# Probabilities transposed two blocks at a time, first loads in turn, and a priority for the norms' mean squares in a two-layer hybrid decoder

## The chip, the cores and the metric

The kernel runs on one NeuronCore of one Trainium2 chip. The metric is the device time of one execution in microseconds (us). A core has five engines that work from queues of their own and wait for each other by semaphores: TensorE (PE: matmuls and transposes; PEld: its weight loads), VectorE (DVE), ScalarE (ACT), GpSimd (POOL) and SyncE (SP), which here issues nearly all loads. An engine's queue runs in order: an instruction that waits holds up everything behind it on that engine. Matmuls write to PSUM, a small memory that ACT and DVE read; everything else lies in SBUF.

## The reference

Two layers, each on 256 positions of width 1024, everything in float32:

```
h = rmsnorm(x);  z = h @ w_in                       # 14 column groups
y_a = nsa(z...) @ w_up_nsa                          # 8 heads, 2 groups: compressed,
                                                    # selected and window branch
y_b = retention(z...) @ w_up_ret                    # 4 heads
x = x + (sigmoid(ma) * y_a + sigmoid(mb) * y_b) @ w_out
x = x + relu(rmsnorm(x) @ w_ff1)**2 @ w_ff2
x = x + sigmoid(rmsnorm(x) @ w_ple_gate) * (p @ w_ple)
```

In the nsa part each of the three branches has a softmax of its own over masked scores, p = e / sum(e), is multiplied by a gate, and the weighted values of the branches are added. With 256 positions the selected branch sees every block, so it is causal attention, and so is the window.

## The kernel before

**Arithmetic.** A float32 matmul is done as three matmuls of a faster type: each operand is split into a high part (`hi`, `XH`, written by ACT) and a rest (`lo`, `XL`, written by DVE as operand minus high part). A weight tile of 128x1024 arrives as `raw`, is split into `hi` and `lo`, and gives 24 matmuls of 256 columns (or 12 of 512).

**Order.** The order on TensorE is written out by the program itself: a main thread takes weight tiles one after the other from a plan and multiplies them ("bulk" below), and background generators (`attend`, `collect`) push small pieces of attention in between. Each piece says by `yield` at which time of a simple model of the engines its inputs should be there; the piece is put on TensorE at the next `poke()` after that. Nothing of this is checked at run time: what is not ready when TensorE comes to it stalls TensorE. On ACT, DVE and POOL a scheduler of the tile library sets the order, and puts instructions under `tc.high_priority()` earlier where it can.

**Attention.** A softmax is done for a pair (g, t) of a head group and a half of the positions, in the order (0,0), (0,1), (1,0), (1,1). `softmax` makes scores (`sc`), exponentials (`e`) and, on POOL, scales `e` block by block with the gate over the sum. `weigh` then takes the blocks (3 for t = 0, 5 for t = 1, one of them only 16 wide, which goes to the tile `PC`). For block i:

- `turn(i)` transposes the four heads' probabilities on TensorE into a PSUM tile `pt` (4 flips). ACT copies it into a tile `pp` (high part), and DVE subtracts that from `pt` into another `pp` (rest).
- `apply(i)` multiplies both `pp` tiles with the values into the accumulator `ot`.

There are two `pt` buffers in turn, so a turn can start only when the DVE subtraction of the turn two before it has read its tile. There are four `pp` buffers, two a block. After the last `apply`, ACT and DVE add the branches up (`o`), and split them (`NHh`, `NHl`). When all four pairs are weighed, `retain` does the last part of retention (`rV`, `rs`, flips of `tmp`).

**Start.** `unit_load` loads the weight tiles; the first tile (plan entry 0) comes in two pieces, and ahead of the first piece stands one load of the first two chunks of x (`XT`). `unit_split(0)` splits, for each piece, one chunk of x and then the piece.

**Norms.** `finish_a` sums squares on TensorE, makes the mean `ms` on DVE and its power `r` on POOL; `finish_b` flips `r` on TensorE.

Of the kernel before, what the change touches and what calls it, by code (L numbers as in the profile page):

```python
# [12 lines left out]
ALU = mybir.AluOpType  # L13
# [4 lines left out]
D = 1024  # L18
# [6 lines left out]
EPS = 1e-6  # L25
# [86 lines left out]
def trunk(ctx: ExitStack, tc: tile.TileContext, xT, wu, wg, cst, msk, par, pin, out):  # L112
# [31 lines left out]
    def p_tile(shape):  # L144
        return ps.tile(shape, F32, tag="pt", name=nm("pt"), bufs=2)

    def o_tile(shape):
        return ps.tile(shape, F32, tag="ot", name=nm("ot"), bufs=1)

    def tmp(shape, dt=F32, tag="tmp", bufs=NTMP):  # L150
        return tp.tile(shape, dt, tag=tag, name=nm(tag), bufs=bufs)
# [7 lines left out]
    def small(shape, tag, bufs=2):  # L159
        return sp.tile(shape, F32, tag=tag, name=nm(tag), bufs=bufs)  # L160
# [3 lines left out]
    cur = [0.0]  # L164

    def width(ap):
        n = 1
        for d in ap.shape[1:]:
            n *= d
        return n  # L170
# [5 lines left out]
    def charge(eng, us):  # L176
        us += 0.03
        if first[0]:
            cur[0] += us + 0.6
            return  # L180
        gs = gaps[eng]
        while len(gs) > 1 and gs[0][1] < vt["pe"] - 6.0:
            gs.pop(0)
        for i, (a, e) in enumerate(gs):
            s = max(a, cur[0])
            if s + us <= e:
                new = []
                if s - a > 0.15:
                    new.append([a, s])
                if e - s - us > 0.15:  # L190
                    new.append([s + us, e])
                gs[i:i + 1] = new
                break
        vt[eng] = gs[-1][0]
        cur[0] = s + us + 0.06

    def fresh(t=None):
        cur[0] = vt["pe"] if t is None else t
# [4 lines left out]
    def act(o, *a, **k):  # L203
        charge("act", 0.1 + width(o) / 1200)
        return nc.scalar.activation(o, *a, **k)  # L205

    def tt(**k):
        charge("dve", 0.07 + width(k["out"]) / 960)
        return nc.vector.tensor_tensor(**k)  # L209

    def ts(**k):
        charge("dve", 0.07 + width(k["out"]) / 960)
        return nc.vector.tensor_scalar(**k)  # L213
# [13 lines left out]
    def gp(**k):  # L227
        n = width(k["out"])
        assert k["op"] in (ALU.pow, ALU.mult, ALU.add)
        charge("pool", (1.1 if n <= 4 else 2.6) if k["op"] == ALU.pow else 0.14 + n / 310)  # L230
        return nc.gpsimd.tensor_tensor(**k)  # L231

    def mm(o, a, b_, **k):
        n = width(b_)
        vt["pe"] += max(n, 64) / 2400 * (4 if b_.dtype == F32 else 1)
        fresh()
        return nc.tensor.matmul(o, a, b_, **k)  # L237

    def flip(o, a, i):
        vt["pe"] += 0.107  # L240
        fresh()
        return nc.tensor.transpose(o, a, i)  # L242

    def sub(out_, a, b):
        tt(out=out_, in0=a, in1=b, op=ALU.subtract)
# [39 lines left out]
    def load_x(a, b_):  # L285
        nc.sync.dma_start(XT[:, a:b_, :], xT[:, a:b_, :])
# [21 lines left out]
    def pair_load(l, i):  # L308


        j = sum(k not in PLAIN for k in range(i))
        B = bp.tile([P, 2, 2, 512], F32, tag=(f"S{2 * l + 1}", f"S{2 * l + 2}", "S7")[j % 3], name="pair")
        for k in range(2):
            nc.sync.dma_start(B[:, k].rearrange("p a b -> p (a b)"), wu[BIG_IX[(l, "ff2", 2 * i + k)]])
        T = bp.tile([P, 3, 512], F32, tag=f"S{5 + j % 2}", name="tsum")
        pairs[l, i] = B, T
# [15 lines left out]
    def unit_load(i):  # L332
        key = PLAN[i]
        if key[1] in PAIR:
            if key[1] == "s2a":
                pair_load(key[0], key[2])
            return
        if key in TWIN:
            h, tag = TWIN[key]
            if h == 0:  # L340
                state["twin"] = bp.tile([P, 2, NW], F32, tag=tag, name=f"raw{i}")
            t = state["twin"][:, h]
        elif key[1] == "w1" or key in EXTRA:
            tag = EXTRA.get(key) or ("B1", "B2", "B5", "B6")[key[2] % 4]
            t = bp.tile([P, NW], F32, tag=tag, name=f"raw{i}")
        else:
            t = wp.tile([P, NW], F32, tag="raw", name=f"raw{i}", bufs=RAW)
        w = spans[i] = 560 if key[1] == "kvg" else NW
        src = wg[KVG_IX[key]] if key[1] == "kvg" else wu[BIG_IX[key]]
        m = w // PIECES.get(key, 1)  # L350
        for c in range(0, w, m):
            if i == 0 and c == 0:
                load_x(0, 2)
            nc.sync.dma_start(t[:, c:c + m], src[:, c:c + m])
        raws[i] = t

# [28 lines left out]
    def advance(i):  # L385
        n = len(PLAN)
        while state["load"] < n and ring[state["load"]] < ring[min(n, i + AHEAD)] + RAW and (
                state["load"] < i + AHEAD + RAW + XA):
            unit_load(state["load"])
            state["load"] += 1  # L390
            load_early(state["load"])
        split_to(i)
# [41 lines left out]
    LATE = 0.9  # L434
# [82 lines left out]
    def finish_a(st):  # L517
        sq = st["sq"]
        pr = p_tile([P, 2])
        for t in range(2):  # L520
            mm(pr[:, t:t + 1], sq[:, 0, t * P:(t + 1) * P], ones, start=True, stop=True)
        ms = small([P, 2], "ms")
        ts(out=ms, in0=pr, scalar1=1.0 / D, scalar2=EPS, op0=ALU.mult, op1=ALU.add)
        r = small([P, 2], "r")
        gp(out=r, in0=ms, in1=mhalf[:, :2], op=ALU.pow)
        st["r"] = r
# [54 lines left out]
    def layer(l, st):  # L581
# [193 lines left out]
        def weigh(g, t):  # L775
            e, blocks, scaled = es.pop((g, t))

            n = len(blocks) - 1
            ot = o_tile([P, HG, P])
            parts = {}  # L780

            def turn(i):
                o, w, b, vv = blocks[i]
                pt = p_tile([P, HG, P])
                for h in range(HG):
                    flip(pt[:w, h, :], e[:, h, o:o + w], ident)
                if w == P:
                    ph = tmp([P, HG, P], F32R, tag="pp", bufs=4)
                    pl = tmp([P, HG, P], F32R, tag="pp", bufs=4)
                else:  # L790
                    ph, pl = PC[:, 0], PC[:, 1]
                act(ph[:w], pt[:w], AF.Copy)
                sub(pl[:w], pt[:w], ph[:w].bitcast(F32))
                parts[i] = ph, pl

            def apply(i):
                o, w, b, vv = blocks[i]
                ph, pl = parts.pop(i)
                mm(ot, vv, ph.rearrange("p a b -> p (a b)"), start=i == 0, stop=False)
                mm(ot, vv, pl.rearrange("p a b -> p (a b)"), start=False, stop=i == n)  # L800

            fin = []
            yield scaled[0]
            turn(0)
            fin.append(cur[0])
            for i in range(1, n + 1):
                yield scaled[i]
                fresh()
                turn(i)
                fin.append(cur[0])  # L810
                yield fin[i - 1]
                apply(i - 1)
            yield fin[n] + LATE
            apply(n)
            on = o2 = tmp([P, 2, P], tag="o", bufs=1)
            ov = ot.rearrange("p (c two) q -> p c two q", two=2)
            act(o2[0:64], ov[64:128, :, 0, :], AF.Copy)
            act(o2[64:128], ov[0:64, :, 1, :], AF.Copy)
            tt(out=on[0:64], in0=ov[0:64, :, 0, :], in1=o2[0:64], op=ALU.add)
            tt(out=on[64:128], in0=ov[64:128, :, 1, :], in1=o2[64:128], op=ALU.add)  # L820
            freed.append(cur[0])
            nh = NHh[:, 2 * g:2 * g + 2, t * P:(t + 1) * P]
            act(nh, on, AF.Copy)
            sub(NHl[:, 2 * g:2 * g + 2, t * P:(t + 1) * P], on, nh.bitcast(F32))
            weighed.add((g, t))
# [173 lines left out]
        for name, u in SEQ[l]:  # L999
# [7 lines left out]
            elif name == "fa":  # L1007
                positions()
                finish_a(st)
                r = st["r"]  # L1010
                rh = small([P, 2], "rh")
# [6 lines left out]
            elif name == "fb":  # L1018
# [3 lines left out]
                    op0=ALU.mult, op1=ALU.mult)  # L1022
# [27 lines left out]
            else:  # L1050
                if name in ("rq", "rk"):
                    i, hp = ("rq", "rk").index(name), u // 2
# [10 lines left out]
                for t in range(2):  # L1063
# [4 lines left out]
                    else:  # L1068
# [4 lines left out]
                            op0=ALU.add, op1=ALU.mult)  # L1073
# [189 lines left out]
        for u in range(2):  # L1263
            for i in range(2):
                b_unit(pms[i], take(l, "fh", 2 * i + u), XH, XL, 4 * u, u == 0, u == 1)
                if u == 1:
                    for q in range(2):
                        ff1_end(2 * i + q, pms[i][:, q])
        finish_a(stf)
        r2 = small([P, 2], "r2")  # L1270
        for i in range(15):
# [39 lines left out]
        for u in range(2):  # L1311
# [3 lines left out]
            for n in range(2):  # L1315
                pm = mm_tile([P, 2, S])
                for k in range(2):
                    for q in range(2):
                        c = (2 * n + q) * P
                        three(pm[:, q, :], vh[:, k, c:c + P], vl[:, k, c:c + P], ph[:, k, :],  # L1320
                              pl[:, k, :], k == 0 and q == 0, k == 1 and q == 1)
                c = 4 * u + 2 * n
# [180 lines left out]
```

## Time and profile before

| | |
|---|---|
| median of 3 runs | 836.47 us (835.97 to 837.29) |
| the profiled execution | 834.93 us |
| its span, first to last instruction | 832.8 us |
| TensorE busy | 823.4 us, 99% of the span |
| VectorE busy | 704.5 us, 85% |
| ScalarE busy | 572.1 us, 69% |
| GpSimd busy | 70.5 us, 8% |

A timeline row has: start (us from the span's start), duration, engine, line, operation, out<-in, shapes, count; in brackets the idle time of the engine before it and what ended it. A row can stand for several equal instructions in a row (x4), and its duration is then from the first start to the last end. Matmuls overlap: one of 256 columns is shown as about 0.28 us long, but the next starts about 0.12 us later; only the distance of the starts tells TensorE's pace. TensorE idle time under 0.15 us is not shown as idle.

### The profile page before, as it was taken

The numbers are of one execution on the slowest core, as the hardware profiler recorded it, in microseconds if no ns is written. First come the engines' busy times: TensorE is split into PE (matmuls) and PEld (weight loads), VectorE is DVE, ScalarE is ACT, GpSimd is POOL, SyncE is SP. The second block draws the span as 40 slices with busy tenths as digits, with TensorE's granted clock in tenths as the row PEclk, the third lists the DMA queues.
The fourth block names the chain that finished last, engine by engine and source line by source line (L and its number), as shares of the span: only waits on it lengthen the run. The fifth ranks groups of instructions, "written<-read, shape, count | busy, mean of one in ns | idle before, by whom it ended". The sixth has DMA issues, their size and how long they took to land.

```text
span 832.8 us, 15190 instructions
## 1 busy us (share of the span) xinstructions
PE 823.4 (99%) x5841; PEld 768.8 (92%) x5841; DVE 704.5 (85%) x1155; ACT 572.1 (69%) x992; POOL 70.5 (8%) x66
## 2 busy tenths in 40 slices
PE   8999999999999999999999999999999999999997
PEld 7998899999999999998999989999999999999897
DVE  7897888787989797979888978886879988989695
ACT  7895977554767676768579868765457677767662
POOL 0410241010000000000003004121000000000000
PEclk9999999999999999999999999999999999999999
DMA  8776453466437474725565654446663565657132
GB/s 319 279 275 211 128 162 127 159 230 240 160 134 245 145 240 148 237 92 203 183 205 172 211 193 135 131 136 205 199 227 129 199 204 178 227 165 239 50 106 74
DMA packets 43560, 152.02 MB, mean 183 GB/s; under 512 B 5088, under 2 KB 5856, under 8 KB 43488
## 3 DMA queue, kind: packets, MB, share of 16 engines
q1 hardware_dynamic: 43344, 151.04, 53.8%
q8 instruction: 46, 0.75, 0.4%
q14 instruction: 26, 0.21, 0.1%
q10 hardware_dynamic: 144, 0.01, 0.0%
HBM read 149.99 MB, written 1.05 MB: 181 GB/s over the span
## 4 chain that ended last, share of the span: by engine, by line
PE 98%; DMA 0%; DVE 0%; ACT 0%; POOL 0%; issue 0%; DVEq 0%; POOLq 0%
PE mm L237 62%; PE sc L237 15%; PE pt L237 10%; PE ot L237 9%; PE pt L242 3%; DMA par<-in_par_dram 0%; PE sc L242 0%; POOL r L231 0%; ACT XH L205 0%; DVE lo L209 0%; ACT hi L205 0%; DVE gz L217 0%; DVE gz L209 0%; DVE XT L209 0%; ACT gz L205 0%
## 5 line engine op out<-in xcount | busy, mean ns | idle before, releaser
L205 ACT ACTIVATE hi<-raw 128x1024 fp32r<-128x1024 f32 (+2 forms) x241 | 248.0, 1041 | 152.7 <-PE mm L237 96.2
L209 DVE TENSOR_TENSOR lo<-raw,hi 128x1024 fp32r<-128x1024 f32 (+2 forms) x241 | 292.3, 1225 | 47.6 <-ACT hi L205 46.7
L237 PE MATMUL mm<-XH,hi 128*128 128x256 f32 x992 | 284.1, 286 | 0.0
L237 PE MATMUL mm<-XH,lo 128*128 128x256 f32 x992 | 280.1, 282 | 0.0
L237 PE MATMUL mm<-XL,hi 128*128 128x256 f32 x992 | 279.1, 281 | 0.0
L237 PEld LDWEIGHTS mm<-XH,hi 128*128 128x128 f32 x992 | 187.1, 189 | 4.4
L237 PEld LDWEIGHTS mm<-XL,hi 128*128 128x128 f32 x992 | 187.2, 189 | 4.2
L237 PEld LDWEIGHTS mm<-XH,lo 128*128 128x128 f32 x992 | 186.9, 188 | 0.0
L209 DVE TENSOR_TENSOR lo<-pair,hi 128x1024 fp32r<-128x1024 f32 x44 | 53.8, 1222 | 14.3 <-ACT hi L205 13.7
L205 ACT ACTIVATE hi<-pair 128x1024 fp32r<-128x1024 f32 x44 | 46.2, 1050 | 16.9 <-PE mm L237 16.5
L231 POOL TENSOR_TENSOR r<-ms,mhalf 128x2 f32<-128x2 f32 x6 | 5.4, 903 | 513.7 <-DVE ms L213 513.7
L209 DVE TENSOR_TENSOR lo<-tsum,hi 128x1024 fp32r<-128x1024 f32 (+1 forms) x44 | 42.0, 954 | 6.4 <-ACT hi L205 6.3
L205 ACT ACTIVATE hi<-tsum 128x1024 fp32r<-128x1024 f32 (+1 forms) x44 | 37.0, 840 | 14.3 <-PE pt L237 9.0
L231 POOL TENSOR_TENSOR e<-e,acf 128x512 f32<-128x512 f32 (+1 forms) x32 | 36.9, 1182 | 113.6 <-DVE acf L209 75.5
L237 PE MATMUL mm<-hi,XH 128*128 128x512 f32 (+2 forms) x128 | 44.4, 347 | 0.0
L237 PE MATMUL mm<-lo,XH 128*128 128x512 f32 (+2 forms) x128 | 43.6, 341 | 0.0
L237 PE MATMUL mm<-hi,XL 128*128 128x512 f32 (+2 forms) x128 | 43.6, 341 | 0.0
L205 ACT ACTIVATE e<-e,nmx 128x128 f32<-128x128 f32 (+2 forms) x96 | 37.6, 393 | 7.4 <-DVE nmx L225 7.4
L205 ACT ACTIVATE ah<-aq 128x896 fp32r<-128x896 f32 (+1 forms) x32 | 29.2, 912 | 11.4 <-DVE aq L209 11.4
L231 POOL TENSOR_TENSOR rso<-rsv,mhalf 128x2 f32<-128x2 f32 (+3 forms) x18 | 25.1, 1398 | 119.5 <-DVE rsv L213 119.4
L209 DVE TENSOR_TENSOR al<-aq,ah 128x896 fp32r<-128x896 f32 (+1 forms) x32 | 33.5, 1046 | 1.9 <-ACT ah L205 1.8
L237 PE MATMUL pt<-hi,ah 128*128 128x512 f32 x84 | 33.2, 395 | 0.0
(226 smaller groups left out, 1767.5 us busy)
## 6 DMA issues: line engine op xcount, KB each, us to landing
raw<-in_wu_dram SPq DMA_DIRECT2D x231, 512.0 KB, 3.9
pair<-in_wu_dram SPq DMA_DIRECT2D x44, 512.0 KB, 4.8
raw<-in_wg_dram SPq DMA_DIRECT2D x8, 280.0 KB, 4.3
cst<-in_cst_dram SPq DMA_DIRECT2D x1, 768.0 KB, 7.5
out_dram<-XT SPq DMA_DIRECT2D x3, 256.0 KB, 2.6
XT<-in_xT_dram SPq DMA_DIRECT2D x2, 256.0 KB, 4.5
raw<-in_wu_dram SPq DMA_DIRECT2D x2, 256.0 KB, 4.2
XT<-in_xT_dram SPq DMA_DIRECT2D x1, 512.0 KB, 6.9
```

The costliest lines, as they stand in the source:

```text
L205: return nc.scalar.activation(o, *a, **k)
L209: return nc.vector.tensor_tensor(**k)
L231: return nc.gpsimd.tensor_tensor(**k)
L237: return nc.tensor.matmul(o, a, b_, **k)
L242: return nc.tensor.transpose(o, a, i)
```

## The change

Three edits.

```
--- unit_load
-            if i == 0 and c == 0:
-                load_x(0, 2)
+            if i == 0:
+                load_x(c // m, c // m + 1)
--- finish_a
-        ts(out=ms, in0=pr, scalar1=1.0 / D, scalar2=EPS, op0=ALU.mult, op1=ALU.add)
+        with tc.high_priority():
+            ts(out=ms, in0=pr, scalar1=1.0 / D, scalar2=EPS, op0=ALU.mult, op1=ALU.add)
--- weigh
-            fin = []
-            yield scaled[0]
-            turn(0)
-            fin.append(cur[0])
-            for i in range(1, n + 1):
-                yield scaled[i]
-                fresh()
-                turn(i)
-                fin.append(cur[0])
-                yield fin[i - 1]
-                apply(i - 1)
-            yield fin[n] + LATE
-            apply(n)
+            fin, last = 0.0, []
+            for i in range(0, n + 1, 2):
+                now = range(i, min(i + 2, n + 1))
+                yield scaled[now[-1]]
+                for j in now:
+                    fresh()
+                    turn(j)
+                due_, fin = fin, cur[0]
+                if last:
+                    yield due_
+                    for j in last:
+                        apply(j)
+                last = now
+            yield fin + LATE
+            for j in last:
+                apply(j)
```

Before, a turn was followed by the apply of the block before it; now two turns are queued together, and the applies of the two blocks before them come after that. The turns of a pair thus go (0 1)(2) or (0 1)(2 3)(4). The instructions are the same in number and shape, but for one more load. Over both layers the order on TensorE changes in the attention stretches alone, and on ACT and DVE there and at the start.

TensorE, the turns of the pair (0,0) in the first layer, before (`pt` is written by the flips, `mm` is bulk, `sc` scores, `ot` an apply):

```order
L242 MATMUL pt_1226<-cst,e_1082 128x128 x4
L237 MATMUL mm_1108<-hi_1069,XH_100 128x512
L237 MATMUL mm_1108<-lo_1070,XH_100 128x512
L237 MATMUL mm_1108<-hi_1069,XL_101 128x512
L242 MATMUL pt_1238<-cst,e_1082 16x128 x4
...
L237 MATMUL sc_1251<-KT_162,qT_169 128x272 x2
L237 MATMUL sc_1254<-KT_162,qT_169 128x256 x2
L237 MATMUL ot_1156<-pp_1231,V_163 128x512
L237 MATMUL ot_1156<-pp_1232,V_163 128x512
L242 MATMUL pt_1273<-cst,e_1082 128x128 x4
```

The same place now:

```order
L242 MATMUL pt_1227<-cst,e_1083 128x128 x4
L242 MATMUL pt_1236<-cst,e_1083 16x128 x4
L237 MATMUL mm_1109<-hi_1070,XH_100 128x512
L237 MATMUL mm_1109<-lo_1071,XH_100 128x512
L237 MATMUL mm_1109<-hi_1070,XL_101 128x512
L242 MATMUL pt_1246<-cst,e_1083 128x128 x4
```

The third turn, which reuses the first turn's `pt`, stood behind six more bulk matmuls, a head's scores and the first apply; now three bulk matmuls lie between the second turn and it, and it has a wait of its own for DVE's subtraction of the first.

DVE, between the last apply of (0,1) and the first subtraction of (1,0), before (`o` and `NHl` belong to (0,1), `lo` is a weight split):

```order
L209 TENSOR_TENSOR lo_1769<-raw_1596,hi_1768 128x1024
L209 TENSOR_TENSOR o_1712<-ot_1376,o_1712 64x256 x2
L209 TENSOR_TENSOR pp_1732<-pt_1726,pp_1731 128x512
L209 TENSOR_TENSOR NHl_166<-o_1712,NHh_165 128x2x128
L225 ISA e_1539,nmx_1540<-sc_1741,masks,nq_171 128x256
```

The same place now:

```order
L209 TENSOR_TENSOR o_1660<-ot_1338,o_1660 64x256 x2
L209 TENSOR_TENSOR lo_1753<-raw_1559,hi_1752 128x1024
L209 TENSOR_TENSOR NHl_167<-o_1660,NHh_166 128x2x128
L209 TENSOR_TENSOR pp_1680<-pt_1674,pp_1679 128x512
L209 TENSOR_TENSOR PC<-pt_1683,PC 16x512
```

The weight split and `NHl` now stand between `o` and the subtraction, where before `o` was followed by it.

SP, the first loads, before:

```order
L286 DMA XT<-in_xT_dram 128x512
L354 DMA raw_102<-in_wu_dram 128x512 x2
L354 DMA raw_106<-in_wg_dram 128x560
L286 DMA XT<-in_xT_dram 128x512
L354 DMA raw_109<-in_wu_dram 128x1024
```

The same now:

```order
L286 DMA XT<-in_xT_dram 128x256
L354 DMA raw_102<-in_wu_dram 128x512
L286 DMA XT<-in_xT_dram 128x256
L354 DMA raw_102<-in_wu_dram 128x512
L354 DMA raw_107<-in_wg_dram 128x560
L286 DMA XT<-in_xT_dram 128x512
L354 DMA raw_110<-in_wu_dram 128x1024
```

One load of two chunks became two of one chunk, each ahead of the piece that goes with it, and everything behind stands one place later.

## Rows read from the trace of the kernel before

**Rows 1.** The page's first part: busy us, share of the span, instructions.

```profile
PE 823.4 (99%) x5841; PEld 768.8 (92%) x5841; DVE 704.5 (85%) x1155; ACT 572.1 (69%) x992; POOL 70.5 (8%) x66
```

**Rows 2.** Who TensorE waited for: us in total, times, longest.

```profile
PE pt L242 <- POOL r L231: 1.5, 1, 1.5
PE sc L237 <- ACT hi L205: 1.5, 1, 1.5
```

**Rows 3.** Chain that ended last, two unbroken pieces (256 and 512 columns): start, us.

```profile
173.63 12.81 PE mm L237 x108
25.27 5.59 PE sc L237 x24
```

**Rows 4.** Busy time by stretch; before the DMA share stands the granted clock.

```profile
85.00:130.00 45.00, 45.00 (x328) 42.22 (x327) 38.15 (x111) 36.82 (x110) 13.15 (x11) 1.00 0.44 137
400.00:412.00 12.00, 10.51 (x89) 10.31 (x89) 9.03 (x14) 5.77 (x8) 1.06 (x1) 1.00 0.78 257
```

**Rows 5.** In order of time, (0,0): two turns, then the first's copy and subtraction.

```profile
93.65 0.60 PE L242 MATMUL pt<-cst,e 128*128 128x128 f32 x4
94.78 0.60 PE L242 MATMUL pt<-cst,e 128*16 128x128 f32 x4
...
95.43 0.58 ACT L205 ACTIVATE pp<-pt 128x512 fp32r<-128x512 f32 x1
...
96.04 0.69 DVE L209 TENSOR_TENSOR pp<-pt,pp 128x512 fp32r<-128x512 f32 x1 [0.23 <-ACT pp L205]
```

**Rows 6.** In order of time, (1,0): a turn whose copy found ACT idle.

```profile
136.99 0.60 PE L242 MATMUL pt<-cst,e 128*128 128x128 f32 x4
...
137.69 0.60 ACT L205 ACTIVATE pp<-pt 128x512 fp32r<-128x512 f32 x1 [0.20 <-PE pt L242]
...
138.32 0.69 DVE L209 TENSOR_TENSOR pp<-pt,pp 128x512 fp32r<-128x512 f32 x1
```

**Rows 7.** In order of time, (1,1): the last apply, and what ACT and DVE do then.

```profile
161.23 0.62 PE L237 MATMUL ot<-pp,V 128*128 128x512 f32 x2
...
161.89 0.77 ACT L205 ACTIVATE o<-ot 64x256 f32<-64x256 f32 x2 [2.06 <-PE ot L237]
162.69 1.06 ACT L205 ACTIVATE hi<-raw 128x1024 fp32r<-128x1024 f32 x1
...
164.19 0.42 DVE L209 TENSOR_TENSOR NHl<-o,NHh 128x256 fp32r<-128x256 f32 x1
164.52 1.22 DVE L209 TENSOR_TENSOR lo<-raw,hi 128x1024 fp32r<-128x1024 f32 x1
```

**Rows 8.** DVE in order of time; two heads' masked scores fill 115.17 to 116.57.

```profile
113.89 1.37 DVE L209 TENSOR_TENSOR pp<-pt,pp 128x512 fp32r<-128x512 f32 x2
115.17 0.34 DVE L225 CUSTOM_DVE_ANT_0 e<-sc,masks,nq 128x128 f32<-128x128 f32 x1
...
116.57 1.22 DVE L209 TENSOR_TENSOR lo<-raw,hi 128x1024 fp32r<-128x1024 f32 x1
```

**Rows 9.** In order of time, retention's second set of flips, and what they read.

```profile
172.11 1.14 DVE L217 SCALAR_TENSOR_TENSOR tmp<-tmp,rso,rG 128x128 f32<-128x128 f32 x4 [0.90 <-POOL rso L231]
...
172.70 0.93 PE L242 MATMUL pt<-cst,tmp 128*128 128x128 f32 x4
```

**Rows 10.** In order of time, the start.

```profile
1.51 3.35 PE L237 MATMUL mm<-warm 128*128 128x512 f32 x7 [1.51 <-DVE warm L280]
4.84 0.91 ACT L205 ACTIVATE XH<-XT,par 128x256 fp32r<-128x256 f32 x2 [2.17 <-DMA par<-in_par_dram]
6.32 0.49 PE L237 MATMUL sc<-hi,XH 128*128 128x512 f32 x1 [1.45 <-ACT hi L205]
10.17 3.04 DVE L209 TENSOR_TENSOR lo<-raw,hi 128x1024 fp32r<-128x1024 f32 x3
11.49 0.46 PE L237 MATMUL sc<-lo,XH 128*128 128x512 f32 x1
11.79 0.39 PE L237 MATMUL sc<-hi,XL 128*128 128x512 f32 x1
```

**Rows 11.** In order of time, the norm before the gate of the first layer.

```profile
408.01 0.15 DVE L213 TENSOR_SCALAR ms<-pt 128x2 f32<-128x2 f32 x1
409.42 0.43 PE L242 MATMUL pt<-cst,r 128*128 128x128 f32 x2 [1.49 <-POOL r L231]
```

## The prediction

> **What bounds the kernel now.** First the page's busy line, which names the engine to look at: TensorE is busy for 99% of the span, the next engine for 85% [rows 1]. Then the list of what TensorE waited for: two waits of 1.5 us and nothing else of that size [rows 2], one at the start, one ahead of a flip of `r`. Then the chain of waits, where the reader sees long unbroken pieces of matmuls; they give TensorE's pace: 12.81 / 108 = 0.119 us for a matmul of 256 columns, 5.59 / 24 = 0.233 for one of 512 [rows 3]. The windows say that in the stretch with all four attention pairs TensorE is busy 45.00 of 45 us at a granted clock of 1.00, its upper level of 2.4 GHz, while VectorE and ScalarE are busy for 38.15 and 36.82 [rows 4]. So a wait that TensorE is spared is worth little, since nearly none is left, and every new wait of TensorE is added whole to the time: no slack lies behind it. The other two engines have 15% and 18% free, but in pieces: what they owe TensorE comes late whenever a longer work stands ahead of it in their queues.
>
> **The norms' mean squares.** `ms` is given a priority, but the instructions of VectorE and GpSimd keep their order around all six of them, so nothing moves: the 1.49 us ahead of the flip of `r` [rows 11] stay. Cost 0. Were it moved ahead as far as it can go, the gain would be that wait at most, and it occurs once.
>
> **First loads.** The first chunk of x now lands alone, and the first piece of weights one place sooner; TensorE's first real matmul, at 6.32, is released by ScalarE's split of a weight piece, behind the split of both chunks of x, 0.91 us for the two [rows 10]. So it may start some 0.45 sooner, half of that. But the same splits of ScalarE must be done before VectorE's `lo` rows, 10.17 to 13.21, and TensorE is at 11.49 and 11.79 already held to their pace: its matmul with `lo` is followed after 0.30 us instead of 0.233 [rows 3, 10]. The second piece, one issue later, keeps its place. What is won at 6.32 is lost by 11.5: 0, with ends of -0.45 (all of it kept) and +0.3 (one more issue in front of everything, the difference being as large as one such gap). The later loads that changed places are of no use before their tiles' splits, many us on: 0, and if that cover failed it would show as a wait for a DMA, which no row of [rows 2] has.
>
> The Trainium skill, page "Perfetto Trace Analysis", section "DMA Optimizations", has two rules for this that pull apart: split transfers let some of them start and finish sooner, while small ones carry more overhead. The first would make the time 0.45 us shorter; by the rows neither decides, because the pace at 11.49 is set elsewhere.
>
> **Turns, what is removed.** Two turns side by side could be cheaper than two apart if the change between flips and bulk had a price. From one turn to the next are 1.13 us, and three matmuls of 512 columns lie between [rows 5]: 1.13 - 3 x 0.233 = 0.43 us for four flips and both changes. I take 0.44 for a turn, side by side or apart. Gain 0.
>
> **Turns, what is added.** There are two `pt`. The third turn of a pair cannot start before VectorE has subtracted the first turn's tile. Before, the apply of that block stood ahead of it in the queue and had waited already, with bulk in between; now only a few matmuls lie between, and TensorE's queue stands still if the subtraction is late: all bulk behind it waits. The cost of each place is the end of that subtraction less the time at which TensorE gets there. The quickest release on record: turn at 136.99, copy at 137.69 with ScalarE waiting for it, subtraction from 138.32 to 139.01, so 2.02 us from a turn's start [rows 6]. Two subtractions in a row end 0.64 apart (115.17 - 113.89 = 1.28 for two [rows 8]).
>
> (0,0), order (0 1) (2): ScalarE and VectorE keep their order up to the first subtraction, which ends at 96.04 + 0.69 = 96.73 [rows 5]. TensorE reaches the third turn after two turns and three matmuls of 512: 93.65 + 2 x 0.44 + 0.70 = 95.23. Wait: **1.5 us**. This is the surest term. If both engines were idle it would still be 2.02 - 1.58 = 0.44.
>
> (0,1), order (0 1) (2 3) (4): TensorE reaches the third turn after 0.88 + 12 x 0.119 = 2.3 us. VectorE has ahead of the first subtraction a copy of `z`, released by a bulk result that ends 13 matmuls (1.55 us) before the first turn, then a weight split, a head's masked scores and another split. A split takes 1.2, two heads' scores 1.40, so one head's 0.7 [rows 8]; with 0.64 for each evacuation the subtraction ends -1.55 + 0.64 + 1.2 + 0.7 + 1.2 + 0.64 = 2.83 us after the turn's start: 0.55 late. The fourth turn, right behind, waits for the second subtraction, some 0.85 later, while its own flips would be reached 0.44 later: 0.4 more. **0.9**, from 0 (nothing ahead on VectorE: 2.02 against 2.3) to 1.8 (one more split of 1.2, less what the fourth turn no longer waits).
>
> (1,0), (0 1) (2): six matmuls ahead of its first turn lies the last apply of (0,1), and VectorE now does a weight split and `NHl` ahead of the first subtraction. The same sequence stands in the rows of (1,1): from the apply's start at 161.23, ScalarE begins `o` 0.66 later, the split's high part 1.46 later and ends it 2.52 later, VectorE ends the low part (1.2) at about 3.75, `NHl` (0.42) at 4.15, and the subtraction (0.64) at 4.8 [rows 7]. TensorE gets to the third turn after the apply's two matmuls, six of bulk, two turns, six of bulk and a head's scores (as long as four matmuls of 256): 0.47 + 0.71 + 0.88 + 0.71 + 0.49 = 3.25. That is 1.55; ScalarE may be held by a head's exponentials beforehand, about as long as VectorE's 0.7, which would make it 2.25. I take **1.8** (1.5 to 2.4, or 0 if the high part of the split goes behind the copy).
>
> (1,1), (0 1) (2 3) (4): the third turn is reached after 0.88 + 0.71 = 1.59 us. No weight split stands ahead of the subtraction, so the quickest release of 2.02 holds [rows 6]: 0.43, and the fourth turn 0.2 behind it (2.66 against 2.46). **0.6** (0.43 to 1.2, if a split comes first after all).
>
> **Retention.** TensorE's second flips of `tmp` take 0.93 instead of 0.60 since VectorE's four products are behind [rows 9]. VectorE has the pair's last work out of the way sooner now, and the flips come later: **-0.3** (-0.33 to +0.3).
>
> Other things moved are hidden: the gate's factors and GpSimd's scaling of a later pair come behind one or two weight splits, 2.4 us, against turns that follow over 10 us later; if that cover failed it would cost the same 2.4 once a pair.
>
> **Sum.** Per layer 1.5 + 0.9 + 1.8 + 0.6 - 0.3 = 4.5, two layers alike: +9.0 us. The profiled execution, 834.93 us (2.1 more than its span), becomes 843.9; it lies 1.5 below the median of the runs, so for the median 836.47 + 9.0 = **845.5 us**. Low end: (0,0) and (1,0) at 1.5 each and (1,1) at 0.43, the others at nothing, -0.3, with the start at -0.45: 2 x 3.1 - 0.45 = 5.8; I go to +4.5, since the copies of a batch could change places on ScalarE. High end: 1.6 + 1.8 + 2.4 + 1.2 + 0.2 = 7.2 per layer, +14.4.
>
> **Rivals.** 0.2% of this time, about 1.7 us, is what a measurement of this kernel can tell from no change.
>
> *Only the two sure places stall.* The scheduler's order leaves (0,1) and (1,0) covered: (1.5 + 0.6 - 0.1) x 2 = +4, 840.5 us. Against it: both have weight splits ahead of the subtraction. Chance 0.06.
>
> *The evacuations keep up.* If the copy and subtraction of each first turn come as fast as at idle engines, (0,0) waits 0.44 and (1,1) 0.43 a layer, the other two nothing: +1.7, less 0.6 for retention and some of the start: +0.7, 837.2, not slower by what can be told. The point from which it decides: the first subtraction ends within about 2 us of its turn's start. For it: [rows 6] shows such a release. Against it: [rows 5] shows one of 3.1 us, at the very place, with the same order ahead. Chance 0.05.
>
> *A gain.* Batches save a change between flips and bulk, the start is 0.45 sooner for good, the 1.49 us wait goes, and no turn waits: 836.47 - 1.9 = 834.5, or less. Against it: 0.43 per turn already without a batch, and an order around `ms` that does not change. Chance 0.02. The Trainium skill would speak for the first part: page "Perfetto Trace Analysis", section "Matmul Optimizations", says that the matmul engine scales its power with use, so matmuls are to be issued back to back in batches. The trace shows a granted clock of 1.00 over the whole stretch [rows 4] with turns apart, so there is nothing left to raise.
>
> *The clock falls.* If each of some eight waits dropped TensorE to its lower level, 1.2 GHz, for as long as the warm-up ran (seven matmuls in 3.35 us instead of 1.63 [rows 3, 10]), that is 1.7 each: +9 + 14 = 859. Against it: the stretch around the existing wait of 1.49 us keeps 1.00 [rows 4]. Chance 0.05.
>
> **How the numbers follow.** The forecast with its own bounds has 0.82, from 841.0 to 850.9. That leaves out the clock, the fast evacuations, the gain and the lower part of the second case, under 0.2 together, so the range stays there. Faster by over 0.2%: 0.02; within 0.2%: 0.05; slower: 0.93.
>
> **What would show it.** In the profile after, TensorE's list of waits should have a new first entry, flips into `pt` that waited for VectorE's `pp`, 10 to 14 times and 8 to 10 us in total, the longest near 1.8; the stretch of the attention should show TensorE busy for some 4 to 5 us less than it lasts, the granted clock still 1.00; the third turn of (0,0) should start at about 96.7; the wait ahead of the flip of `r` should stand at 1.5 unchanged; the first matmul should start at 5.9 to 6.3 with no gain left at 12. Wrong it would be if those flips start within some 2 us of the batch's first turn, if ScalarE takes the copy ahead of a weight's high part, or if the time goes where no turn is.

## The result: 848.23 us, 1.5% slower

| | before | after |
|---|---|---|
| median (runs shown together) | 836.22 us | 848.23 us |
| lowest to highest | 834.76 to 837.29 | 847.13 to 849.42 |
| ratio, 95% interval | | 1.0147, 1.0135 to 1.0159 |
| the profiled execution | 834.93 | 847.13 |
| its span | 832.8 | 845.2 |

TensorE still bounds the kernel, but it is no longer packed. The page's busy line of after, answering to [rows 1]:

```profile
PE 828.2 (98%) x5841; PEld 770.6 (91%) x5841; DVE 700.5 (83%) x1155; ACT 571.5 (68%) x992; POOL 63.3 (7%) x66
```

The list of TensorE's waits, answering to [rows 2] (who waited <- for whom: us in total, times, longest):

```profile
PE pt L242 <- DVE pp L209: 7.8, 6, 2.1
PE mm L237 <- DVE warm L280: 1.5, 1, 1.5
PE pt L242 <- DVE acf L213: 0.9, 2, 0.5
PE sc L237 <- DVE lo L209: 0.8, 1, 0.8
PE pt L242 <- POOL r L231: 0.7, 1, 0.7
PE sc L237 <- ACT hi L205: 0.3, 1, 0.3
```

The first entry is new: flips into `pt` that wait for VectorE's subtraction, six times, 7.8 us. The third entry belongs to it: the wait at (0,1), where the two subtractions and a small `acf` instruction stand together on VectorE, is put down to the `acf`. The windows give the same by place; in the columns each engine has its busy us, and the granted clock stands before the DMA share. The two windows hold the attention of the first and of the second layer, 74 us each:

```profile
92.00:166.00 74.00, 69.50 (x527) 65.36 (x526) 55.65 (x139) 50.62 (x128) 16.39 (x16) 1.00 0.36 117
508.00:582.00 74.00, 69.50 (x527) 65.37 (x526) 55.74 (x139) 50.65 (x128) 16.40 (x16) 1.00 0.33 116
```

TensorE is idle for 4.50 us in each. [rows 4] ends at 130 us, ahead of the turns of (1,0) and (1,1); a stretch of the kernel before that is as long and holds all four pairs has no idle time:

```profile
90.00:164.00 74.00, 74.00 (x578) 71.14 (x577) 60.56 (x137) 52.84 (x130) 18.56 (x16) 1.00 0.43 137
```

The granted clock is 1.00 in all three. TensorE's busy time is the same in both layers after, to the last digit: this is an order that repeats, not noise.

**Where the 12.4 us of the two spans lie.** The first turn of (0,0) starts 2.53 us later than before (96.18 against 93.65 in [rows 5]): lost at the start. The flip of `r` in the first layer starts 7.22 later (416.64 against 409.42 in [rows 11]); it waits 0.73 instead of 1.49, so without that it would be 7.98 later, and 7.98 - 2.53 = 5.45 came from the first layer's attention. The rest, 12.4 - 7.22 = 5.2, is the second layer's. Where one cuts moves a tenth or two: at the second layer's first turn (512.16 against 505.07, 7.09 later) the layers come to 5.3 each.

### The four pairs in the trace after

A timeline row is read as in front. (0,0): the first two turns (x8 flips), ScalarE's copy and VectorE's subtraction of the first, the third turn.

```profile
96.18 1.04 PE L242 MATMUL pt<-cst,e 128*128 128x128 f32 x8
...
97.96 0.57 ACT L205 ACTIVATE pp<-pt 128x512 fp32r<-128x512 f32 x1
...
98.57 0.69 DVE L209 TENSOR_TENSOR pp<-pt,pp 128x512 fp32r<-128x512 f32 x1 [0.23 <-ACT pp L205]
...
99.40 0.63 PE L242 MATMUL pt<-cst,e 128*128 128x128 f32 x4 [1.49 <-DVE pp L209]
```

TensorE is there at 96.18 + 0.88 + 0.70 = 97.76 and starts at 99.40: 1.64 us. The subtraction ends 3.08 us after the first turn's start, to the hundredth what [rows 5] had (96.73 - 93.65): with the same order ahead of it, the sequence took the time that it took in the trace of before.

(1,0), the longest: a head's exponential on ScalarE, `o` of (0,1), the first two turns, the weight split's high part, the copy, the split's low part, `NHl`, the subtraction, the third turn.

```profile
130.52 0.49 ACT L205 ACTIVATE e<-e,nmx 128x256 f32<-128x256 f32 x1
...
131.12 0.77 ACT L205 ACTIVATE o<-ot 64x256 f32<-64x256 f32 x2
131.12 1.03 PE L242 MATMUL pt<-cst,e 128*128 128x128 f32 x8
...
131.91 1.06 ACT L205 ACTIVATE hi<-raw 128x1024 fp32r<-128x1024 f32 x1
...
132.88 0.58 ACT L205 ACTIVATE pp<-pt 128x512 fp32r<-128x512 f32 x1
133.00 1.22 DVE L209 TENSOR_TENSOR lo<-raw,hi 128x1024 fp32r<-128x1024 f32 x1 [0.23 <-ACT hi L205]
...
134.15 0.42 DVE L209 TENSOR_TENSOR NHl<-o,NHh 128x256 fp32r<-128x256 f32 x1
...
134.60 0.69 DVE L209 TENSOR_TENSOR pp<-pt,pp 128x512 fp32r<-128x512 f32 x1
...
135.44 0.63 PE L242 MATMUL pt<-cst,e 128*128 128x128 f32 x4 [2.07 <-DVE pp L209]
```

The copy is done at 133.46, yet the subtraction begins at 134.60: it stands behind the split and `NHl`. TensorE is there at 131.12 + 0.88 + 0.71 + 0.49 = 133.20 and starts at 135.44: 2.24 us.

(0,1) and (1,1), in each the first two turns, and the third and fourth (x8 flips):

```profile
117.60 1.04 PE L242 MATMUL pt<-cst,e 128*128 128x128 f32 x8
...
120.52 1.35 PE L242 MATMUL pt<-cst,e 128*16 128x128 f32 x8 [0.46 <-DVE acf L213]
...
153.33 1.04 PE L242 MATMUL pt<-cst,e 128*128 128x128 f32 x8
...
155.43 1.23 PE L242 MATMUL pt<-cst,e 128*16 128x128 f32 x8 [0.35 <-DVE pp L209]
```

At (0,1) TensorE is there at 117.60 + 2.30 = 119.90 and starts at 120.52, 0.62 late; the eight flips then take 1.35 instead of 1.04, since the fourth turn waits too: 0.93 us together. At (1,1) it is there at 153.33 + 1.59 = 154.92 and starts at 155.43, 0.51 late, and 0.19 for the fourth turn: 0.70. The third turn starts 2.10 us after the first here, near the 2.02 of [rows 6].

### The profile page after: what moved, and what is told of

It is laid out like the page before. It is cut to its first block, busy times and chain, and to the rows that moved or that the text cites. A ratio compares the mean times of both kernels' runs of the same rounds, so it can differ in the third digit from the quotient of the medians.

```text
span 845.2 us, 15187 instructions
## 1 busy us (share of the span) xinstructions
PE 828.2 (98%) x5841; PEld 770.6 (91%) x5841; DVE 700.5 (83%) x1155; ACT 571.5 (68%) x992; POOL 63.3 (7%) x66
## 4 chain that ended last, share of the span: by engine, by line
PE 94%; DVE 2%; ACT 2%; DMA 1%; issue 1%; SPq 0%; POOL 0%; POOLq 0%
PE mm L237 59%; PE sc L237 14%; PE pt L237 10%; PE ot L237 8%; PE pt L242 2%; DMA XT<-in_xT_dram 1%; DVE lo L209 1%; DVE pp L209 1%; ACT e L205 1%; ACT hi L205 0%; DVE e L225 0%; PE sc L242 0%; ACT pp L205 0%; ACT o L205 0%; SPq L354 0%
## 5 line engine op out<-in xcount | busy, mean ns | idle before, releaser
L209 DVE TENSOR_TENSOR lo<-raw,hi 128x1024 fp32r<-128x1024 f32 (+2 forms) x241 | 289.4, 1212 | 53.7 <-ACT hi L205 52.7
L205 ACT ACTIVATE e<-e,nmx 128x128 f32<-128x128 f32 (+2 forms) x96 | 37.6, 394 | 10.8 <-DVE nmx L225 10.7
L231 POOL TENSOR_TENSOR e<-e,acf 128x512 f32<-128x512 f32 (+1 forms) x32 | 32.8, 1055 | 120.5 <-DVE acf L209 87.3
L225 DVE CUSTOM_DVE_ANT_0 e<-sc,masks,nq 128x128 f32<-128x128 f32 (+2 forms) x96 | 29.0, 350 | 7.3 <-PE sc L237 7.1
```

Source lines behind the costliest of these rows:

```text
L225: return nc.vector.tensor_tensor_reduce(**k)
```

## Experiments

The kernel before was run beside each. Ratios are against it, with a 95% interval.

### The three edits apart

**First loads alone.**

```
-            if i == 0 and c == 0:
-                load_x(0, 2)
+            if i == 0:
+                load_x(c // m, c // m + 1)
```

> The kernel before with the change to the first loads alone. Theory (from the trace after, where the first real matmul started 1.17 us sooner and TensorE was 2.53 us later from 16 us on): the two loads of one chunk slow the first transfers, chunks 2 and 3 of x land over 2 us later, and TensorE waits for their splits near 13 us: +2.5 us, about 838.7. Rival: what the trace after shows at its start is one execution's chance and the edit costs nothing, as forecast: within 1 us of before, and chunks 2 and 3 land before 8 us.

836.75 us against 836.13, ratio 1.0010 (1.0000 to 1.0021). The late landing was there again, with a full TensorE pace this time, so it is not the one execution's chance; but the time rose by only 0.6, with an interval that begins at no change. Both theories are half right; the start has its own section below.

**Turns alone.** The diff of `weigh` in front, and nothing else.

> The kernel before with the turns two at a time alone. Theory: the third and fourth turns wait for VectorE's subtraction of the turn two before, 5.4 us a layer as in the trace after: +10.9 us, about 847.1, with six waits of over 0.3 us, the longest 2.1 at (1,0). Rival: part of the 5.4 a layer is brought about by the other two edits (loads that stand otherwise, DMA times): then under +9 us.

847.42 us against 836.13: +11.3, ratio 1.0132 (1.0118 to 1.0146). The six waits for the subtraction are there with the same total, 7.8 us, and the same longest, 2.1. The turns are the loss, without help of the other edits.

**Priority alone.**

```
-        ts(out=ms, in0=pr, scalar1=1.0 / D, ...)
+        with tc.high_priority():
+            ts(out=ms, in0=pr, scalar1=1.0 / D, ...)
```

> The kernel before with the priority for the mean squares alone. Theory: the order on VectorE and GpSimd is the same, so this is the same program: 0 us, the wait ahead of the flip of r in the first layer stays near 1.5 us. Rival: the shorter wait of 0.7 us that the trace after shows there comes from the priority: -0.8 us, and a wait of 0.7 here too.

836.23 us against 836.13, ratio 0.9995 (0.9986 to 1.0004). TensorE's list has the wait still, 1.4 us:

```profile
PE pt L242 <- POOL r L231: 1.4, 1, 1.4
```

The edit does nothing. The 0.7 in the trace after is not its work: with the same instruction order the wait was 1.2 in the kernel with the turns alone and 1.7 in that with the loads alone, both without the priority. The medians of the three, +0.6, +11.3 and +0.1, make +12.0, which is the whole.

### Is it the pairs, or the place of the third turn?

**Pairs, queued in time.** The generator waits, in the order's model, for the subtraction that frees the tile:

```
-                yield scaled[now[-1]]
+                yield max([scaled[now[-1]]] + ends[max(0, i - 2):][:len(now)])
                 for j in now:
                     fresh()
                     turn(j)
+                    ends.append(cur[0])
```

> Turns two at a time alone, but each group of turns is queued only when the written-out order's model says that the subtractions of the turns two before are done; the third turn then stands behind more bulk. Theory: the missing wait in the order is the whole cause, so the waits for subtractions fall under 0.3 us each and the time is that of before within 1.5 us. Rival: doing turns in pairs costs in itself (two evacuations at once on ScalarE and VectorE push the weight splits and the scores back): +3 us or more, with waits that name other work than the subtraction.

836.15 us against 836.13, ratio 1.0000 (0.9991 to 1.0008). The list of waits has no turn in it any more. (0,0) in its trace: the two turns still together, and the third now behind more bulk and a head's scores.

```profile
93.75 1.03 PE L242 MATMUL pt<-cst,e 128*128 128x128 f32 x8
...
96.14 0.69 DVE L209 TENSOR_TENSOR pp<-pt,pp 128x512 fp32r<-128x512 f32 x1 [0.23 <-ACT pp L205]
...
97.21 0.60 PE L242 MATMUL pt<-cst,e 128*128 128x128 f32 x4
```

The subtraction ends at 96.83 and the third turn comes at 97.21, no longer waiting. Pairs cost nothing and bring nothing that can be told; what cost 11.3 us was where the third turn stood.

**Another tile for the third turn.** Same order on TensorE, but the third turn (and the fourth of the pairs of five blocks) takes a bank of the scores:

```
-                pt = p_tile([P, HG, P])
+                pt = (p_tile if i < 2 or i == 4 else s_tile)([P, HG, P])
```

> Turns two at a time alone, in the same order on TensorE, but the third turn of a pair (and the fourth of the pairs of five) goes into a bank of the scores instead of reusing the first turn's tile; so it needs no subtraction of its own pair. Theory: the wait belongs to the reused tile, so at (0,0), (0,1) and (1,1) the waits vanish (1.65 + 0.91 + 0.68 = 3.2 us a layer); at (1,0) the score just ahead uses that bank and VectorE reads it after the first subtraction, so some 2 to 3 us stay there, now named as a wait for a score's reader; later scores may wait a few tenths. About 847.4 - 6.4 + 1.5 = 842.5. Rival: the order of VectorE and ScalarE alone makes the loss, whatever the tile: 847 again.

855.9 us against 836.34: +19.6, ratio 1.0236. A clear miss: slower still, where a gain of some 5 us on the turns alone had been expected. The mechanism shows nevertheless. At (0,0) the third turn starts at once, and the wait goes to the next score, which needs that bank; at (1,0) it is longer than it was:

```profile
95.31 0.60 PE L242 MATMUL sc<-cst,e 128*128 128x128 f32 x4
...
96.44 0.41 PE L237 MATMUL sc<-KT,qT 128*128 128x272 f32 x2
...
98.05 0.51 PE L237 MATMUL sc<-KT,qT 128*128 128x256 f32 x2 [1.19 <-DVE pp L209]
...
136.09 1.09 PE L242 MATMUL sc<-cst,e 128*128 128x128 f32 x4 [3.21 <-DVE nmx L225]
```

TensorE's granted clock, in front of the DMA share in the rows below, fell to half three times: in the first layer during the wait of 3.21 us; in the second after two waits, of 0.97 and 0.83 us, close together, for the scores of (0,1), and again during a wait of 3.22. The same two waits in the first layer, of 0.94 and 0.83, left it at 1.00: the first row is the stretch behind them. In the other two rows, behind the wait of 3.21 and behind the two of the second layer, TensorE had work throughout and did it at 1.2 GHz for most of the time:

```profile
123.70:127.20 3.50, 3.50 (x26) 3.23 (x25) 2.02 (x5) 2.73 (x6) 0.00 (x0) 1.00 0.02 9
...
138.00:140.80 2.80, 2.80 (x15) 2.80 (x14) 0.59 (x1) 0.00 (x0) 0.00 (x0) 0.50 0.00 0
...
544.70:548.20 3.50, 3.50 (x17) 3.11 (x15) 0.89 (x2) 1.55 (x4) 0.00 (x0) 0.55 0.00 0
```

So the waits lie with the tile, as thought, but a tile borrowed from another rotation passes the wait on. The expectation had counted a few tenths for the scores; they waited 0.8 to 1.2 each. This kernel's list has 13.0 us of waits for turns and scores, of the 19.6; that the lower clock makes up the rest was not summed. The Trainium skill, page "Perfetto Trace Analysis", section "Optimization Strategy", says that the same gap repeating on the engine that should be saturated can mean too little SBUF or PSUM for the next tile; the gap repeats in both layers here, and yet, by the run before this one, no more PSUM was needed, only another place in the order.

### The start, and TensorE's pace there

TensorE's pace differs between executions of one order. In the trace of the kernel with the turns alone, which has the old first loads, TensorE ran the warm-up, idled 1.74 us, began at full pace and fell to 0.43 us for a matmul of 512 columns, the rate of 1.2 GHz:

```profile
6.49 0.50 PE L237 MATMUL sc<-hi,XH 128*128 128x512 f32 x1 [1.74 <-ACT hi L205]
...
7.56 0.39 PE L237 MATMUL sc<-hi,XL 128*128 128x512 f32 x1
7.78 0.51 PE L237 MATMUL sc<-hi,XH 128*128 128x512 f32 x1
8.09 0.63 PE L237 MATMUL sc<-lo,XH 128*128 128x512 f32 x1
8.52 0.63 PE L237 MATMUL sc<-hi,XL 128*128 128x512 f32 x1
```

It stayed there to 11.1. The kernel with the priority alone had the slow stretch too; the profiled execution of before did not. The first turn of (0,0) starts at 95.31, 95.37 and 93.65 in the three: the slow stretch costs 1.7 us, half of the spread of the kernel before over 27 runs (834.26 to 837.58). The Trainium skill, page "TensorE: Matmul & The Clock Gate", section "Part 1: The HAM clock gate", says that the number of slow matmuls at a program's start varies from run to run; these traces agree: in that of before only the seven of the warm-up were slow, in the other two some seven or eight more.

**Small loads in the old order.**

```
             if i == 0 and c == 0:
-                load_x(0, 2)
+                load_x(0, 1)
+                load_x(1, 2)
```

> The kernel before with x's first two chunks as two loads of one chunk, both ahead of the first weight piece (the old order of the data, the new size of the loads). Theory: the loads of 1 KB a partition, and one issue more, slow the transfers that follow, as in both executions with the new first loads: chunks 2 and 3 land at about 10 us instead of 7.6 and TensorE is at 51.9 us where it was at 49.4 to 51.1: +0.6 us. Rival: the interleaving of x and the weights does it: then these land at 7.6 to 8 and the time is that of before within 0.4 us.

836.10 us against 836.34, ratio 0.9999 (0.9990 to 1.0008). In the trace chunks 2 and 3 landed late here too, so it doesn't take the interleaving for that; in time the edit is within the noise. The trace is of the slowest of this kernel's 11 executions (837.26), so it may not stand for all of them. ScalarE's split of these chunks, waiting for the load, in after, with the new loads alone, and here:

```profile
10.28 0.91 ACT L205 ACTIVATE XH<-XT,par 128x256 fp32r<-128x256 f32 x2 [1.56 <-DMA XT<-in_xT_dram]
```

```profile
10.20 0.91 ACT L205 ACTIVATE XH<-XT,par 128x256 fp32r<-128x256 f32 x2 [1.14 <-DMA XT<-in_xT_dram]
```

```profile
9.79 0.91 ACT L205 ACTIVATE XH<-XT,par 128x256 fp32r<-128x256 f32 x2 [2.23 <-DMA XT<-in_xT_dram]
```

In the trace of before it started at 7.77, without a wait:

```profile
7.77 0.89 ACT L205 ACTIVATE XH<-XT,par 128x256 fp32r<-128x256 f32 x2
```

SyncE issues this load at 3.06 in these three and at 2.58 in before, so its later place in the queue can account for 0.5 us of the 2.5. The first turn of (0,0) starts at 96.18, 96.12 and 96.28 in these three, at the fast pace as at the slow: with the late data it no longer matters how fast TensorE is ahead of them. That makes +2.5 against a start without the slow stretch and +0.8 against one with it.

**A longer warm-up.** `NWARM` 11 instead of 7.

> The kernel before with 11 instead of 7 warm-up matmuls, so that TensorE has no idle 1.5 us ahead of its first real matmul. Theory: the stretch in which matmuls of 512 columns take 0.43 us instead of 0.23, seen from 7 to 11 us in two of four traces with the old first loads, follows from that idle time; without it the pace is full from the first real matmul on in nearly every execution: -1.2 us in the median, 835.0, and a narrower spread of the runs (2.0 us instead of 3.3). Rival: the slow stretch does not depend on the idle time: no change, or slower by up to 0.5 us where the warm-up itself is at the slow pace and delays the first matmul.

834.69 us against 836.34, ratio 0.9985 (0.9976 to 0.9994); the spread is 2.2 us (834.06 to 836.26). Its trace has no idle time ahead of the first real matmul and full pace from 7.3 on:

```profile
6.37 0.68 PE L237 MATMUL sc<-hi,XH 128*128 128x512 f32 x1
6.98 0.50 PE L237 MATMUL sc<-lo,XH 128*128 128x512 f32 x1
7.32 0.39 PE L237 MATMUL sc<-hi,XL 128*128 128x512 f32 x1
7.55 0.40 PE L237 MATMUL sc<-hi,XH 128*128 128x512 f32 x1
```

The gain fits the theory: of the nine traces with 7 warm-up matmuls four have the slow stretch, of the three with 11 none. That idle time alone sets the pace doesn't follow: the trace after idled only 0.28 there and was slow to 10.7, and before idled 1.45 and was not.

### The wait for r, removed for good

```
-                if u == 1 and j == 0:
+                if u == 0 and j == 2:
                     finish_a(stp)
```

> The kernel before with the sums, mean and power of the norm ahead of the gate put one weight tile (24 matmuls, 2.9 us) sooner on TensorE. Theory: in the first layer the mean stood behind a weight split on VectorE and cost TensorE 1.5 us; with the sums sooner it comes ahead of that split: -1.5 us, 834.6, and no wait for r. Rival: the mean is put behind a split again and the flips of r still wait: 0.

834.40 us against 836.34, ratio 0.9976 (0.9966 to 0.9986). The gain of 1.94 is 0.4 more than the wait in the trace of before, which lies within the interval. `ms` now comes 4.5 us ahead of the flips, and these don't wait:

```profile
403.13 0.15 DVE L213 TENSOR_SCALAR ms<-pt 128x2 f32<-128x2 f32 x1
...
407.66 0.38 PE L242 MATMUL pt<-cst,r 128*128 128x128 f32 x2
```

**Both gains together**, and both with the pairs queued in time. The two diffs above, and the last two with that of `weigh`.

> The kernel before with 11 warm-up matmuls and the norm's sums one weight tile sooner, and none of the three edits. Theory: the two gains lie at different places and add, -1.4 and -1.7: 833.0 us, with no wait of TensorE over 0.5 us after the first 8 us. Rival: what is won at the start is given back at the next weight loads, or the wait for r was partly there for other reasons: then only one of the two, about 834.5.

> The same with the turns two at a time, queued when the model says that the subtractions of the turns two before are done. Theory: pairs of turns bring nothing in themselves, so the time is that of the kernel with the two gains alone, 833.0 within 1 us. Rival: pairs free TensorE of the 0.3 us that retention's flips wait for in each layer: -0.6 us.

833.32 and 833.10 us against 835.97, ratio 0.9974 (0.9963 to 0.9984) and 0.9974 (0.9963 to 0.9985). Neither list of waits has one over 0.5 us but the one ahead of the warm-up. The gains add for the most part, 2.7 and 2.9 of 1.65 + 1.94, and pairs add nothing that can be told. These two are faster than both kernels of this document.

## Why the prediction was right, and where it was off

**The turns: right in mechanism and nearly in size.** Place by place, the prediction and the trace after:

| | forecast | measured |
|---|---|---|
| (0,0) | 1.5 | 1.64 |
| (0,1) | 0.9 | 0.93 |
| (1,0) | 1.8 | 2.24 |
| (1,1) | 0.6 | 0.70 |
| retention | -0.3 | -0.33 |
| sum per layer | 4.5 | 5.2 |

The second flips of retention take 0.60 now instead of the 0.93 in [rows 9]. Two sizes were off. One is small and in each place: the forecast let the flip start when the subtraction ends, and it starts 0.14 to 0.15 us later in all four, as at (0,0) (98.57 + 0.69 = 99.26 against 99.40). At (0,0) that is the whole difference. The larger is in (1,0): the end at 1.55 assumed that ScalarE is free when the last apply of (0,1) ends. It was still in a head's exponentials until 131.1, so `o` and the split began late; the text had named that case, 2.25, and chose a value in the middle. What is left between 5.2 and the 5.3 or 5.45 of the first layer is not assigned. In the medians the turns cost 11.3 us, against the forecast's 9.0.

One row was read wrongly without harm: [rows 4] ends at 130 and holds two of the four pairs, not all; the stretch with all four shows the same, 74.00 busy of 74 us.

**The priority: right.** Forecast 0, measured 0.1 with an interval on both sides of none.

**The first loads: the step failed, in its reason more than in its size.** The forecast said that the first matmul would start 0.45 us sooner at most, that this would be lost to the pace of the splits by 11.5, and that the later loads are covered. In the trace after it started 1.17 sooner (5.15 against 6.32), since ScalarE's first split started at 3.98 instead of 4.84 and was of one chunk. It was lost, but to loads: chunks 2 and 3 landed 2.5 us later than in before, their split came first on ScalarE, and TensorE waited near 13 for both parts of the weight split behind it. ScalarE's high parts, and TensorE's first matmul with the low part, in after (in before it stands at 11.49 [rows 10]):

```profile
11.62 1.60 ACT L205 ACTIVATE hi<-raw 128x1024 fp32r<-128x1024 f32 x2
...
13.98 0.50 PE L237 MATMUL sc<-lo,XH 128*128 128x512 f32 x1 [0.76 <-DVE lo L209]
```

"The later loads are of no use before their tiles' splits, many us on" was wrong for the very next load. The range of the term ended at +0.3; the median moved by 0.6 and the profiled execution by 2.5. The Trainium skill, page "Perfetto Trace Analysis", section "DMA Optimizations", warns that small transfers carry overhead; the prediction set this aside as deciding nothing, and the traces came out on that side: with 1 KB a partition in the first loads chunks 2 and 3 came later in three of three. That the overhead is what delayed them is not shown.

**The sum against one execution.** The profiled execution of before was among the fastest of its kernel because TensorE had no slow stretch at its start. A sum against it is safe for what lies later, but what an edit does to the start can't be read from one execution.

**The signs.** The new first entry, the idle time of 4.5 us, the clock of 1.00 and the third turn of (0,0) (99.40, so 96.87 without the 2.53 of the start) came as foretold. The entries are 8 with those put down to the `acf`, not 10 to 14. The wait for `r` stood at 0.73, not 1.5, and the first matmul at 5.15, not 5.9 to 6.3.

**The rivals.** That the evacuations keep up fell at (0,0), where the release took 3.08 us as in [rows 5]. That only two places stall fell with (1,0). That batches gain fell with the pairs queued in time, 836.15 against 836.13. The clock did not fall here, though the run with the scores' banks shows that it can.

## What to carry to other kernels

When an order is written out by hand for an engine that never idles, each item needs its full list of what it waits for, the tile that it reuses among them: pairs of turns cost 11 us until the order knew of the second reason to wait, and nothing after. Here a release time copied from the trace of before held to a tenth where the work ahead of it kept its order, and was off where another engine's queue was assumed free; the step from the release to the released instruction, 0.14 us, belongs in the sum as well. The priority on one instruction changed no order here; issuing its inputs one tile sooner moved it.

## What was not expected of the hardware

Two loads of 1 KB a partition in place of one of 2 KB, at the very start, go with slower loads behind them. The last column of the windows is what the core moved in GB/s; here from 6 to 8 us, of before and of after:

```profile
6.00:8.00 2.00, 1.45 (x5) 1.01 (x6) 1.62 (x4) 2.00 (x5) 0.00 (x0) 1.00 1.00 400
```

```profile
6.00:8.00 2.00, 2.00 (x5) 1.61 (x6) 0.91 (x2) 0.65 (x2) 0.00 (x0) 1.00 0.94 280
```

The DMA engines are about as busy and move 280 instead of 400. Why is open: the size of the loads, their number, and what they collide with by landing sooner were not told apart. How often it costs time is open too: the lowest runs with small loads lie 1.3 and 1.5 us above the lowest of before beside them, the medians -0.2 and +0.6. The same rows show that the granted clock can stand at 1.00 while the pace is the lower one: in after, matmuls of 512 columns were 0.43 us apart there, which only the distance of their starts tells:

```profile
6.90 0.63 PE L237 MATMUL sc<-hi,XH 128*128 128x512 f32 x1
7.33 0.63 PE L237 MATMUL sc<-lo,XH 128*128 128x512 f32 x1
```

In the kernel with the scores' banks TensorE's clock fell during both waits of 3.2 us, and after two waits of about 1 us in one layer but not in the other; in after it kept 1.00 with waits of up to 2.24 us. A new wait can so cost more than its length; here it didn't.
